# Memory stage at the head of a two-layer decoder: load order, sums of squares and the split of work over DVE and POOL changed

## The chip, the core and the metric

The kernel runs on one core of a Trainium2 chip. TensorE (PE in the profile, with its weight loads as PEld), VectorE (DVE), ScalarE (ACT), GpSimd (POOL) and SyncE (SP, whose queue issues nearly all DMAs here) run side by side, each through its own list of instructions in order, and wait for one another through semaphores. The metric is the device time of one execution in microseconds, the median of several runs.

## The reference

Two layers over 512 positions of width 1024: a gated-DeltaNet layer, then a sliding-window attention layer. Each layer also attends with four heads into 256 fixed memory rows. What the change touches is the start of it all:

```python
mem_n = rms_norm(mem, ln_mem)                 # (256, 1024)
for layer in range(DEPTH):
    h = rms_norm(x, ln_mix[layer])            # (512, 1024)
    mkv = mem_n @ w_mem_kv[layer]
    mem_k, mem_v = mkv[..., :256], mkv[..., 256:]
    ...
def rms_norm(x, g):
    y = x * rsqrt(mean(x * x, axis=-1) + EPS)
    return y * g
```

The keys and values of the memory for both layers, and the norm of x for the first layer, are therefore due before the first large projection (`h @ w_in`).

## The kernel before

**Layout.** Everything is kept transposed: the 1024 features lie as eight tiles of 128 partitions (`KD` = 8), the positions along the free axis (512 for x, 256 for mem). A product in f32 accuracy is made of three products of the faster fp32r type: each operand is split into a high part (an fp32r copy on ACT, `whi`, `mh`, `h`) and a low part (the difference, on DVE, `wlo`, `ml`, `l`), and `mm3` (L190) adds high x high, high x low and low x high. One weight tile of 128 x 1024 is a raw load (`wraw`, L173), an ACT copy and a DVE subtraction (`weight`, L179, in `parts` pieces), then 24 products.

**Norms.** The norm's factor is one number per position. `rstd_of` (L210) squares the eight feature tiles on ACT, adds them in pairs on DVE, and sums over partitions with four products by a matrix of ones on PE, in plain f32; then Ln and Exp on ACT (`rsqrt`, L205) give mean-square to the power -1/2. The factor of the memory (`mr`) is not put on mem itself: keys are multiplied by it on the way out of PSUM, values by its transpose, two columns `mc` that `memory_columns` (L373) makes on PE. The factor of x (`xr`) is multiplied into x together with the gain, one DVE instruction for each of eight tiles (`norm`, L350), then each tile is split.

**The stage.** `mem_and_norm` (L283) issues the loads on SP: gains (in `load_constants`, L258), mem in four pieces with the first key weight in two halves between them, the second key weight, the constants and a small table, x in four pieces of 512 KB, the two value weights of layer 0, `wab` (the weight of the gates), and the four memory weights of layer 1. Weight loads of the first large projection (`in_win`) follow. It then computes keys of layer 0 (two tiles in PSUM tiles `pj`), the sums of squares (PSUM `g`), values of layer 0, keys of layer 1 (PSUM `sc`), values of layer 1, and the norm of x. Results for layer 1 (`kt`) are stored to DRAM (`keep`, L380). `gates` (L392) follows with products of `h`, `l` and `wabs`, a selection by a constant matrix (`g<-consts,ab`), a short chain on DVE and ACT that ends in `gate`, and products by `gate`. Then come the projections `normed(m)`, 24 products each.

A scheduler of the language decides where each instruction stands on its engine; the order in the source is its starting point. Buffers rotate in pools: six raw weights (`wraw`), three high and three low weights, six squares (`sq`).

Of the kernel before, what the change touches and what calls it, by code (L numbers as in the profile page):

```python
# [9 lines left out]
F32 = mybir.dt.float32  # L10
# [3 lines left out]
ALU = mybir.AluOpType  # L14
# [4 lines left out]
P = 128  # L19
T = 512  # L20
D = 1024
KD = D // P
# [21 lines left out]
C_ID, C_U, C_ONE, C_CAUS, C_BAND = 0, 128, 256, 384, 512  # L44
C_SEL, C_INV, C_SIGN = 768, 780, 781
C_N = 782
# [20 lines left out]
def constants():  # L67
# [4 lines left out]
    c[:, C_ONE:C_ONE + P] = 1.0  # L72
# [13 lines left out]
class Builder:  # L86
# [123 lines left out]
    def rstd_of(self, tiles, pool, out, after=None):  # L210

        ps = self.bank("g")[:, :tiles[0].shape[1]]
        for k in range(0, KD, 2):
            two = []
            for x in tiles[k:k + 2]:
                sq = self.t(pool, [P, x.shape[1]], F32, "sq", 6)
                two.append(sq)
                ins = self.square(sq, x)
                if after is not None:
                    self.nosync(ins, after)  # L220
            self.tt(self.nc.vector, two[0], two[0], two[1], ALU.add)
            self.mm(ps, self.ones, two[0], k == 0, k == KD - 2)
        self.rsqrt(out, ps, D)
# [34 lines left out]
    def load_constants(self, cp):  # L258
# [4 lines left out]
        nc.sync.dma_start(g, a["gains"])  # L263
# [3 lines left out]
        self.ones = c[:, C_ONE:C_ONE + P]  # L267
        self.caus = c[:, C_CAUS:C_CAUS + P]
        self.band = c[:, C_BAND:C_BAND + 2 * P]
        self.one = c[:, C_ONE:C_ONE + 1]  # L270
# [12 lines left out]
    def mem_and_norm(self, ep):  # L283
# [9 lines left out]
        for k in range(0, KD, 2):  # L293
            nc.sync.dma_start(mem[:, k:k + 2, :], a["memT"][:, k:k + 2, :])
            if k < 4:
                s = slice(k // 2 * T, (k // 2 + 1) * T)
                nc.sync.dma_start(raw[0][:, s], a["wmk"][0, 0][:, s])
        raw += [early(a["wmk"][0, 1])]
        self.fetch_constants()
# [4 lines left out]
        raw += [early(s) for s in (a["wmv"][0, 0], a["wmv"][0, 1])]  # L304
        wab = self.t(ep, [P, KD, 12], F32, "wab")
        nc.sync.dma_start(wab, a["wab"])
        raw += [early(s) for s in (a["wmk"][1, 0], a["wmk"][1, 1], a["wmv"][1, 0], a["wmv"][1, 1])]
# [54 lines left out]
        keys(1)  # L362
        values(1)
        norm()
# [864 lines left out]
```

## Time and profile before

| what | value |
|---|---|
| runs of the kernel | 1167.21, 1167.46, 1170.11 us, median 1167.46 |
| the profiled execution | 1169.1 us, of which the span of the instructions is 1167.3 us |
| granted TensorE clock | 0.996 |
| PE busy | 1144.1 us |
| DVE, ACT, POOL busy | 834.2, 629.4, 82.9 us |

Rows of the timeline read: start in us, duration in us, engine, line, operation, tile written <- tiles read, shape, count, and in brackets the idle time of the engine before it with what ended it. Rows of groups give a count, then total busy us and mean ns of one, then idle time before. Rows of the table of windows give the stretch, its length, and busy time and count for PE, PEld, DVE, ACT and POOL in it, then the granted clock, the DMA share and GB/s. The chain of waits goes back from the last instruction to what released each step; its rows are start, duration, and what. Durations of products on PE include their way through the array, so the distance between two starts is what one costs.

### The profile page before, as it was taken

What the parts mean: (1) busy time and instruction counts of PE and PEld (TensorE: products, weight loads), DVE (VectorE), ACT (ScalarE), POOL (GpSimd) and SP (SyncE); (2) the same over time, 40 slices, a digit from 0 to 9 for tenths busy, and PEclk for the clock granted to TensorE, in tenths of its full rate; (3) what the DMA queues carried; (4) which work ended last, traced back from release to release, by engine and by line L of the source; (5) the groups of instructions that cost most, each with busy time, mean ns of one, the idle gap of its engine ahead of it and who ended that gap; (6) DMA issues with size and microseconds to landing.
All of it is one profiled execution on the core that took longest, in us unless ns stands there. A gap on an engine that the chain in (4) does not pass through costs nothing.

```text
span 1167.3 us, 19448 instructions
## 1 busy us (share of the span) xinstructions
PE 1144.1 (98%) x7410; PEld 999.2 (86%) x7410; DVE 834.2 (71%) x1558; ACT 629.4 (54%) x1250; POOL 82.9 (7%) x93
## 2 busy tenths in 40 slices
PE   7999999999999999999999999999999999999996
PEld 6888777877889998899998877688999988999986
DVE  6654877767788876488965768758788734889654
ACT  7579564366466642256643546865566422566433
POOL 0210000000011101011100000010011000111000
PEclk9999999999999999999999999999999999999998
DMA  8334352224557735467623421153477633776232
GB/s 306 126 110 113 114 127 92 72 91 162 163 136 187 175 102 155 123 165 180 163 79 99 129 82 55 37 126 110 100 189 183 155 99 106 168 171 172 76 99 84
DMA packets 72944, 151.22 MB, mean 130 GB/s; under 512 B 16732, under 2 KB 19444, under 8 KB 72852
## 3 DMA queue, kind: packets, MB, share of 16 engines
q1 hardware_dynamic: 61908, 130.06, 36.3%
q0 software_dynamic: 10944, 19.93, 10.9%
q8 instruction: 58, 0.95, 0.4%
q14 instruction: 34, 0.28, 0.1%
HBM read 143.00 MB, written 6.96 MB: 128 GB/s over the span
## 4 chain that ended last, share of the span: by engine, by line
PE 91%; ACT 4%; DVE 3%; DMA 1%; issue 0%; SPq 0%; DVEq 0%; ACTq 0%
PE pj L143 44%; PE g L143 39%; PE sc L143 6%; ACT sm L131 1%; PE g L147 1%; PE pt L147 1%; DVE wlo L150 1%; ACT sm L137 1%; DMA wraw<-in_wmk 1%; ACT whi L137 0%; ACT T L137 0%; PE qk L143 0%; DVE mx L743 0%; DVE sm L739 0%; DMA wraw<-in_wdn 0%
## 5 line engine op out<-in xcount | busy, mean ns | idle before, releaser
L137 ACT ACTIVATE whi<-wraw 128x512 fp32r<-128x512 f32 (+3 forms) x325 | 243.1, 754 | 292.3 <-PE pj L143 191.4
L150 DVE TENSOR_TENSOR wlo<-wraw,whi 128x512 fp32r<-128x512 f32 (+3 forms) x325 | 271.9, 845 | 109.0 <-ACT whi L137 103.5
L143 PE MATMUL pj<-h,whi 128*128 128x512 f32 (+1 forms) x676 | 265.9, 394 | 0.2
L143 PE MATMUL pj<-l,whi 128*128 128x512 f32 (+1 forms) x676 | 265.2, 392 | 0.0
L143 PE MATMUL pj<-h,wlo 128*128 128x512 f32 (+1 forms) x676 | 264.4, 392 | 0.0
L143 PE MATMUL g<-T,whi 128*128 128x256 f32 x1216 | 220.5, 282 | 0.0
L143 PEld LDWEIGHTS g<-T,whi 128*128 128x128 f32 x1216 | 187.0, 189 | 1.1 <-DVE fu L153 1.1
L143 PE MATMUL g<-T,wlo 128*128 128x256 f32 x608 | 171.1, 281 | 0.0
L143 PE MATMUL g<-h,whi 128*128 128x256 f32 (+1 forms) x516 | 152.8, 296 | 0.0
L143 PE MATMUL g<-h,wlo 128*128 128x256 f32 (+1 forms) x516 | 152.0, 295 | 0.0
L143 PE MATMUL g<-l,whi 128*128 128x256 f32 (+1 forms) x516 | 151.8, 294 | 0.0
L143 PEld LDWEIGHTS pj<-h,whi 128*128 128x128 f32 x676 | 127.1, 188 | 28.4 <-issue 2.7
L143 PEld LDWEIGHTS pj<-h,wlo 128*128 128x128 f32 x676 | 127.2, 188 | 27.2 <-issue 2.2
L143 PEld LDWEIGHTS pj<-l,whi 128*128 128x128 f32 x676 | 127.2, 188 | 26.3 <-issue 1.2
L143 PEld LDWEIGHTS g<-T,wlo 128*128 128x128 f32 x608 | 114.4, 188 | 0.0
L143 PEld LDWEIGHTS g<-h,whi 128*128 128x128 f32 x516 | 98.0, 190 | 2.9 <-issue 0.2
L143 PEld LDWEIGHTS g<-l,whi 128*128 128x128 f32 x516 | 97.9, 190 | 2.9 <-issue 0.5
L143 PEld LDWEIGHTS g<-h,wlo 128*128 128x128 f32 x516 | 98.0, 190 | 2.4
L978 POOL DMA_DIRECT2D ws<-in_wgu x38 | 33.6, 883 | 735.1 <-DVE wlo L150 335.3
L137 ACT ACTIVATE whi<-ws 128x512 fp32r<-128x512 f32 x76 | 48.0, 631 | 49.3 <-PE g L143 41.2
L150 DVE TENSOR_TENSOR fu<-pj,rstd 128x512 f32<-128x512 f32 (+1 forms) x34 | 22.4, 660 | 53.0 <-PE pj L143 53.0
L150 DVE TENSOR_TENSOR wlo<-ws,whi 128x512 fp32r<-128x512 f32 x76 | 52.1, 686 | 7.3 <-ACT whi L137 7.2
(346 smaller groups left out, 1626.0 us busy)
## 6 DMA issues: line engine op xcount, KB each, us to landing
wraw<-in_wgu SPq DMA_DIRECT2D x50, 512.0 KB, 4.1
ws<-in_wgu SPq DMA_DIRECT2D x76, 256.0 KB, 3.5
ws<-in_wgu POOLq DMA_DIRECT2D x76, 256.0 KB, 4.9
wraw<-in_win SPq DMA_DIRECT2D x26, 512.0 KB, 3.6
wraw<-in_wdn SPq DMA_DIRECT2D x32, 384.0 KB, 3.2
wraw<-in_wdn SPq DMA_DIRECT2D x32, 320.0 KB, 2.9
wraw<-in_wgu SPq DMA_DIRECT2D x38, 256.0 KB, 4.6
wraw<-in_wout SPq DMA_DIRECT2D x16, 512.0 KB, 3.6
```

The source lines that it names most:

```text
L131: ins = self.nc.scalar.activation(out, in_, func, **kw).ins
L137: self.copied = self.nc.scalar.activation(out, in_, AF.Copy, **kw).ins
L143: return self.nc.tensor.matmul(out, lhsT, rhs, start=start, stop=stop, skip_group_check=more).ins
L147: return self.nc.tensor.transpose(out, in_, self.ident[:k, :k]).ins
L150: return eng.tensor_tensor(out=out, in0=a, in1=b, op=op).ins
L978: nc.gpsimd.dma_start(s1, a22, accum_op=ALU.add)
```

## The change

Five things change, all in the first 45 us.

- **Loads.** The first piece of mem goes ahead of the gains. Both value weights of layer 0 and the first key weight of layer 1 go ahead of x; the constants and the small table go last. The matrix of ones is no longer among the constants but is set on DVE.
- **Sums of squares.** DVE adds the eight squares one after the other; PE makes one product by ones in place of four. The squares of x come after the values of layer 0.
- **The second key tile of layer 0.** Its weight is split in two halves, and its eight products with the low part of the weight stand last.
- **Low parts on POOL.** The second value weight of layer 0 gets its low part on POOL in place of DVE. (The test `j > layer` holds for that one alone.)
- **x's factors.** For four of the eight tiles, POOL multiplies x by `xr`, and the gain comes in with the split (ACT copy with a scale, DVE multiply and subtract). The norm of x stands ahead of the values of layer 1 in the source.

In the order that the scheduler makes of it, PE runs: key tile 0, key tile 1, two products of the first value tile, the product by ones for mem, ten value products, the columns, the rest of the value tiles, 18 products of layer 1's first key tile, the product by ones for x, the other layer-1 key products, 14 products of each layer-1 value tile, nine of the gates' products, two of the first projection, and then what the last value weight's low part allows: the other ten of each value tile, seven gates' products, the projections. On ACT the first value weight's copy stands behind the eight squares of mem, and a copy of a layer-1 key weight between Ln and Exp of `mr`; the last square of x stands behind the copy of the second value tile. On SP the `in_win` loads stand behind the first store of layer 1's keys.

```diff
@@ rstd_of
-        for k in range(0, KD, 2):
-            two = []
-            for x in tiles[k:k + 2]:
-                sq = self.t(pool, [P, x.shape[1]], F32, "sq", 6)
-                two.append(sq)
-                ins = self.square(sq, x)
-                if after is not None:
-                    self.nosync(ins, after)
-            self.tt(self.nc.vector, two[0], two[0], two[1], ALU.add)
-            self.mm(ps, self.ones, two[0], k == 0, k == KD - 2)
+        acc = None
+        for x in tiles:
+            sq = self.t(pool, [P, x.shape[1]], F32, "sq", 6)
+            ins = self.square(sq, x)
+            if after is not None:
+                self.nosync(ins, after)
+            if acc is not None:
+                self.tt(self.nc.vector, sq, acc, sq, ALU.add)
+            acc = sq
+        self.mm(ps, self.ones, acc)
@@ load_constants
-        nc.sync.dma_start(g, a["gains"])
-        self.ones = c[:, C_ONE:C_ONE + P]
+        self.ones = self.t(cp, [P, P], F32, "ones")
+        nc.vector.memset(self.ones, 1.0)
@@ mem_and_norm
             nc.sync.dma_start(mem[:, k:k + 2, :], a["memT"][:, k:k + 2, :])
+            if k == 0:
+                nc.sync.dma_start(self.gains, a["gains"])
...
-        raw += [early(a["wmk"][0, 1])]
-        self.fetch_constants()
+        raw += [early(s) for s in (a["wmk"][0, 1], a["wmv"][0, 0], a["wmv"][0, 1], a["wmk"][1, 0])]
...
             nc.sync.dma_start(x[:, k:k + 2, :], a["xT"][:, k:k + 2, :])
-        raw += [early(s) for s in (a["wmv"][0, 0], a["wmv"][0, 1])]
+        raw += [early(a["wmk"][1, 1])]
         wab = self.t(ep, [P, KD, 12], F32, "wab")
         nc.sync.dma_start(wab, a["wab"])
-        raw += [early(s) for s in (a["wmk"][1, 0], a["wmk"][1, 1], a["wmv"][1, 0], a["wmv"][1, 1])]
+        raw += [early(s) for s in (a["wmv"][1, 0], a["wmv"][1, 1])]
+        self.fetch_constants()
@@ keys
-                w = self.weight(None, nc.vector, raw[4 * layer + m], 1 if m + layer else 2)
+                w = self.weight(None, nc.vector, raw[4 * layer + m], 1 if layer else 2)
+                if m and not layer:
+                    s = lambda k: slice(k * P, (k + 1) * P)
+                    for k in range(KD):
+                        self.mm(ps[m], w[0][:, s(k)], mh[:, k, :], k == 0, False)
+                        self.mm(ps[m], w[0][:, s(k)], ml[:, k, :], False, False)
+                    for k in range(KD):
+                        self.mm(ps[m], w[1][:, s(k)], mh[:, k, :], False, k == KD - 1)
+                    continue
@@ values
-            w = [self.weight(None, nc.vector, raw[4 * layer + 2 + j]) for j in range(2)]
+            w = [self.weight(None, nc.gpsimd if j > layer else nc.vector, raw[4 * layer + 2 + j]) for j in range(2)]
@@ norm
-                self.stt(xk, xk, self.gain(G_MIX[0], k), xr, ALU.mult, ALU.mult)
-                self.split(xk, *self.h[k])
+                if k % 2:
+                    self.tt(nc.gpsimd, xk, xk, xr, ALU.mult)
+                    self.split_gain(xk, self.gain(G_MIX[0], k), *self.h[k])
+                else:
+                    self.stt(xk, xk, self.gain(G_MIX[0], k), xr, ALU.mult, ALU.mult)
+                    self.split(xk, *self.h[k])
@@ the order of the calls
         self.memK = keys(0)
-        self.rstd_of([x[:, k, :] for k in range(KD)], ep, xr)
         self.memory_columns(mr, mc)
         self.memV = values(0)
+        self.rstd_of([x[:, k, :] for k in range(KD)], ep, xr)
         keys(1)
+        norm()
         values(1)
-        norm()
```

More of the change, by code (lines that the diff above doesn't have):

```diff
@@ L41 @@
 G_N = G_GDN + 1
-C_ID, C_U, C_ONE, C_CAUS, C_BAND = 0, 128, 256, 384, 512
-C_SEL, C_INV, C_SIGN = 768, 780, 781
-C_N = 782
+C_ID, C_U, C_CAUS, C_BAND = 0, 128, 256, 384
+C_SEL, C_INV, C_SIGN = 640, 652, 653
+C_N = 654
 INV_FREQ = [float.fromhex(s) for s in (
@@ L71, in constants @@
     c[:, C_U:C_U + P] = i[:, None] <= i[None, :]
-    c[:, C_ONE:C_ONE + P] = 1.0
     c[:, C_CAUS:C_CAUS + P] = np.where(i[None, :] >= i[:, None], 0.0, NEG)
@@ L266, in load_constants @@
         self.U = c[:, C_U:C_U + P]
-        self.ones = c[:, C_ONE:C_ONE + P]
+        self.ones = self.t(cp, [P, P], F32, "ones")
+        nc.vector.memset(self.ones, 1.0)
         self.caus = c[:, C_CAUS:C_CAUS + P]
         self.band = c[:, C_BAND:C_BAND + 2 * P]
-        self.one = c[:, C_ONE:C_ONE + 1]
+        self.one = self.ones[:, 0:1]
         v = self.t(cp, [P, 2], F32, "eps")
```

## The prediction

> **What bounds the kernel now.** I read the page first: the span and the busy shares.
>
> ```profile
> span 1167.3 us, 19448 instructions
> PE 1144.1 (98%) x7410; PEld 999.2 (86%) x7410; DVE 834.2 (71%) x1558; ACT 629.4 (54%) x1250; POOL 82.9 (7%) x93
> ```
>
> PE is busy for all but 23.2 us, so a microsecond of PE work or PE waiting that disappears is a microsecond of the span, and other engines matter only where PE waits for them. The diff ends with the memory stage, so next I read the table of windows and the chain of waits there.
>
> ```profile
> 28.30:43.50 15.20, 15.20 (x114) 13.76 (x113) 14.56 (x21) 8.95 (x14) 3.54 (x4) 1.00 0.20 60
> ```
> ```profile
> 10.76 1.07 ACT whi L137
> ...
> 11.85 1.24 DVE wlo L150
> ...
> 13.13 2.89 PE pj L143 x22
> 16.02 6.01 PE g L143 x20
> ...
> 28.50 8.64 PE sc L143 x72
> ```
>
> From 28.3 us on PE is full. The chain shows 8.64 us for 72 products: 0.12 us from one 256-column product to the next, so about 0.24 for 512 columns. Before that the chain leaves PE at 10.76 to 13.13 (copy, then subtraction of a key weight), and spends 6 us in g, the sums of squares by ones. PE's timeline shows the pieces.
>
> ```profile
> 12.09 0.28 PE L143 MATMUL pj<-ml,whi 128*128 128x256 f32 x1
> ...
> 13.13 0.39 PE L143 MATMUL pj<-mh,wlo 128*128 128x256 f32 x1 [0.76 <-DVE wlo L150]
> ...
> 15.86 3.60 PE L143 MATMUL g<-sq,consts 128*128 128x256 f32 x12
> ```
> ```profile
> 18.44 1.02 PE L143 MATMUL g<-sq,consts 128*128 128x512 f32 x2
> ```
> ```profile
> 18.87 0.59 PE L143 MATMUL g<-sq,consts 128*128 128x512 f32 x1
> 19.39 0.60 PE L143 MATMUL g<-consts,mr 1*128 1x1 f32 x4
> ```
> ```profile
> 21.98 0.28 PE L143 MATMUL pj<-whi,ml 128*128 128x256 f32 x1
> ...
> 24.57 0.28 PE L143 MATMUL pj<-whi,mh 128*128 128x256 f32 x1
> 25.01 0.39 PE L143 MATMUL pj<-wlo,mh 128*128 128x256 f32 x1 [0.16 <-DVE wlo L150]
> ```
>
> A plain f32 product stands as two passes. Two 512-column passes start 0.43 apart (18.44, 18.87), so 256 columns take 0.215: eight of these and two of 0.43 are 2.58 us, just the distance from 15.86 to 18.44. The g stretch, 15.86 to 21.98, is 6.12 us: 8 x 0.215 + 8 x 0.43 = 5.16 of sums, 0.60 for the two columns of mr, 0.36 of waiting. PE also waits 13.13 - 12.09 - 0.12 = 0.92 for the low part of the second key weight, and 25.01 - 24.57 - 0.12 = 0.32 for that of a value weight.
>
> **The change, part by part.** Durations of the other engines, from the groups by shape within the first 50 us, and for POOL from the whole span:
>
> ```profile
> L150 DVE TENSOR_TENSOR wlo<-wraw,whi 128x1024 fp32r<-128x1024 f32 x10 | 12.2, 1223 | 4.9 <-ACT whi L137 4.8
> L137 ACT ACTIVATE whi<-wraw 128x1024 fp32r<-128x1024 f32 x10 | 10.6, 1056 | 3.0 <-PE sc L143 1.8 <-PE pj L143 0.9 <-DMA wraw<-in_wmk 0.2
> ...
> L153 DVE SCALAR_TENSOR_TENSOR x<-x,gains,xr 128x512 f32<-128x512 f32 x8 | 5.8, 746 | 0.0
> ...
> L150 DVE TENSOR_TENSOR sq<-sq,sq 128x512 f32<-128x512 f32 x4 | 2.8, 692 | 2.7 <-ACT sq L140 2.7
> ...
> L150 DVE TENSOR_TENSOR sq<-sq,sq 128x256 f32<-128x256 f32 x4 | 1.6, 422 | 0.2 <-ACT sq L140 0.2
> ...
> L137 ACT ACTIVATE whi<-wraw 128x512 fp32r<-128x512 f32 x2 | 1.2, 612 | 0.0
> ```
> ```profile
> L150 POOL TENSOR_TENSOR DT<-gcr,consts 128x512 f32<-128x512 f32 x6 | 8.5, 1458 | 10.6 <-DMA gcr<-dr 10.6
> ...
> L150 POOL TENSOR_TENSOR T<-T,ws 128x512 f32<-128x512 f32 x2 | 2.6, 1284 | 89.0 <-ACT ws L131 89.0
> ```
>
> (1) One product by ones in place of four, for mem and for x: six 256-column and six 512-column passes go, 6 x 0.215 + 6 x 0.43 = **3.87 us of PE work removed**. The 0.36 of waiting among them goes too.
>
> (2) The second key weight is cut in halves and its low products stand last. The copy halves end at about 11.4 and 11.9 (0.61 each from 10.76), the low halves on DVE (0.69 each) at 12.1 and 12.7. PE ends the first key tile at 12.0 and has 16 high products, to 13.9, before it needs a low part. The wait of 0.92 goes; the tile ends at 14.85 instead of 15.86. With the 0.32 above, whose place in the new order is worked out in (4), the removed waits are 0.92 + 0.36 + 0.32 = **1.6 us**.
>
> (3) Loads. The memory weights stand ahead of x on SP, the constants last.
>
> ```profile
> GB/s 0 38 139 227 193 326 338 389 375 400 304 311 390 373 426 414 426 407 417 417 406 410 414 414 410 348 205 20 0 0 0 0 36 103 0 125 6 8 131 0
> ```
> ```profile
> 5.46 0.91 ACT L137 ACTIVATE mh<-mem,gains 128x256 fp32r<-128x256 f32 x2 [3.44 <-DMA mem<-in_memT]
> ...
> 17.79 0.47 ACT L131 ACTIVATE mr<-g,eps 128x256 f32<-128x256 f32 x1
> ```
> ```profile
> 17.87 1.61 SPq L176 DMA_DIRECT2D wraw<-in_win  x2
> 32.06 3.06 SPq L384 DMA_DIRECT2D mk<-kt  x2
> ```
> ```profile
> wraw<-in_win SPq DMA_DIRECT2D x26, 512.0 KB, 3.6
> ```
>
> The row of rates (40 slices of 1 us) runs near 410 GB/s, 1.28 us for 512 KB. Both orders bring the second key weight at 10.7; then come the value weights at 12.0 and 13.3, a layer-1 key weight at 14.6, x at 15.9, 17.1, 18.4 and 19.7, the rest by about 25. Constants are first read near 41 us (gates), the ones now come from a DVE memset: both cost nothing. Gains swap places with the first part of mem, and the first ACT copy needs both: between 0.44 earlier (one issue slot, mem's) and 0.3 later; I take 0, since the same bytes are ahead of the pair. The win loads fall behind the store of mk on SP. That store waits for the first layer-1 key tile, near 27.5; a load then takes 3.6 us, so the first is there at 31.5 and the second at 32.3, and ACT's copies of them stand behind the fourth h, which ends at 32.6: covered, by a microsecond or less.
>
> (4) New waits. ACT is in order:
>
> ```profile
> 11.72 2.55 ACT L140 ACTIVATE sq<-mem 128x256 f32<-128x256 f32 x8
> ```
>
> A: the eight squares (2.55) start at 11.8 and end at 14.35, the value weight's copy behind them at 15.35; PE, done at 14.85, waits 0.5. B: seven dependent adds of 0.42 + 0.02 on DVE run from 12.6 to 15.7, after which PE's one product takes 0.43, to 16.15 (wait 0.1); the value weight's low part stands behind the adds on DVE, 15.6 to 16.85: PE waits 0.7. The columns need Ln 0.47, a layer-1 key copy of 1.06 that stands between, and Exp: 18.1, where PE arrives as well (0.05). C: the second value weight's low part is now on POOL. It starts at 16.3; 128x1024 is not in the trace, twice the 512 rows gives 2.57 to 2.92, ending 18.9 to 19.2, and PE asks at 18.95: 0 to 0.3, I take 0.15. New waits so far 0.5 + 0.1 + 0.7 + 0.05 + 0.15 = **1.5**. The lead at layer 1's first key product is 3.87 + 1.6 - 1.5 = 4.0 us; x's product (0.86) is still to come there, so this product moves from 28.5 to about 23.6.
>
> The Trainium skill ("GPSIMD Engine Reference", Performance versus the Vector engine) gives POOL 1.96 times DVE's time for an f32 tensor_tensor; on DVE's 1.223 that would be an estimated 2.40 us, C would be 0 and the sum 0.15 better.
>
> x's chain: the eighth square queues on ACT behind the second value tile's copy, which waits for PE until 23.6; its add ends at 25.4, and PE, 18 products further, asks for the sum at 25.8: covered, by 0.4. Then 0.86 on PE, Ln, a weight copy, Exp: xr at 29.0. D: half of x's factors move to POOL (four times 1.28 to 1.46, from 29.0 to 34.8 at most). DVE saves four of 0.746. It still has, in this order from 28.4, a value weight's low part, two x, a kt (as the 256-column add, 0.42), four l, two x and the last value weight's low part. On DVE instructions overlap:
>
> ```profile
> 36.00 1.89 DVE L150 TENSOR_TENSOR l<-x,h 128x512 fp32r<-128x512 f32 x3
> ```
>
> Three of 0.69 in 1.89: 0.09 at each border. So 2 x 1.223 + 6 x 0.746 + 2 x 0.69 + 0.42 = 8.7, less 0.9 at ten borders, ends near 36.2. PE, with 12.5 us of products behind 23.6, asks for that low part at 36.1. DVE beside POOL:
>
> ```profile
> 55.47 8.53 POOL L150 TENSOR_TENSOR DT<-gcr,consts 128x512 f32<-128x512 f32 x6 [10.56 <-DMA gcr<-dr]
> ```
> ```profile
> 57.73 1.36 DVE L150 TENSOR_TENSOR wlo<-wraw,whi 128x1024 fp32r<-128x1024 f32 x1 [0.89 <-ACT whi L137]
> ```
>
> With POOL at work the subtraction took 1.36 instead of 1.223, 11% more; on 5 us of overlap that is 0.5. So D is between 0.1 and 1.2 (the stretch doubled); I take **0.5**. E, the gates:
>
> ```profile
> 45.56 0.51 PE L143 MATMUL pj<-l,whi 128*128 128x512 f32 x1
> 45.91 0.40 PE L143 MATMUL pj<-h,wlo 128*128 128x512 f32 x1
> ```
> ```profile
> 47.99 0.18 DVE L153 SCALAR_TENSOR_TENSOR gate<-gate,ea 128x24 f32<-128x24 f32 x1
> ```
>
> From the end of the gates' selection (45.56) to the gate (48.17) are 2.6 us; the new order puts 8 products of about 0.24 there, 1.9 us: a wait of 0 to 0.7, I take **0.3**. F: a change between plain f32 and fp32r products costs 0.35 - 0.24 = 0.1 (45.56 to 45.91). The sums now stand in three places instead of one: two more visits, 0 to 0.4, **0.2**.
>
> Sum: 4.0 - 0.5 - 0.3 - 0.2 = **3.0 us** off. The profiled execution took 1169.1 (span 1167.3 and 1.8 around it), so it would be 1166.1; it stands 1.6 above the median of the runs, 1167.46, from which the same 3.0 gives **1164.5**. I carry the lead to the end in full, since PE's other waits start from results that come earlier by as much. Bounds of the unknown costs: best 4.0 + 0.15 + 0.44 - 0.1 = 4.5, so 1163.0; worst 4.0 - 0.15 - 0.3 - 1.2 - 0.7 - 0.4 = 1.25, so 1166.2.
>
> **The rivals.** (R1) More than the sum: A and B do not come to pass. Both hang on a DVE chain of seven adds and on ACT's place for one copy; were these a microsecond earlier, PE would find its operands, and 3.0 + 1.2 = 4.2 gives 1163.3, with the best of the other bounds 1161.9. Against it: ACT's 2.55 us of squares are a row, and they stand ahead of the copy. (R2) The lead is swallowed: the win loads issued ten microseconds later, or x's chain with its 0.4 of cover, become the wait. Each microsecond that one is late is lost; 2 to 3 us late, which a load of 3.6 that meets others can be, gives 1166.5 to 1167.5. For it: the covers of a microsecond and less; against: the row of rates falls to 0 at 28 us, the queue is empty there. (R3) Slower: DVE and POOL shut each other out of SBUF for a whole instruction. Then in D each of POOL's four multiplications holds DVE, whose operations all have two SBUF inputs, for 1.28 to 1.46 us: 5.1 to 5.8 on a chain without slack. 4.0 - 0.3 - 0.2 - (5.1 to 5.8) is 1.6 to 2.3 us slower: 1169.1 to 1169.8, and more if POOL waits for DVE as well. It decides from 3.5 us of lost DVE time on. Against it: the subtraction at 57.73 began in the middle of six POOL operations without a break and took 0.13 longer, no POOL operation's length.
>
> The rule behind R3 is the Trainium skill's ("SBUF — State Buffer", Who interferes with whom): a DVE instruction with two SBUF inputs and a GpSimd one that reads SBUF exclude each other, "an exclusive lock". By that rule 57.73 should have waited for the running POOL operation; the trace doesn't show it.
>
> **How the numbers follow.** Forecast 0.58, R1 0.15, R2 0.17, R3 0.10. The likeliest is 1164.5, with its own range of 1163.0 to 1166.2; taking in R2 and most of R1, 1162.0 to 1167.4 leaves out under 2 in 10. About 0.3%, 3.5 us, is what a measurement of this kernel can tell from no change: faster is under 1163.96, slower over 1170.96. Faster: R1's 0.15 and a little under half of the forecast, 0.27, so 0.42. Slower: half of R3, 0.05. Within: 0.53.
>
> **What would show it.** Right: two products by ones of two passes each; no wait at the second key tile; waits of 0.5 and 0.7 for a value weight's copy and low part near 15 and 17 us; layer 1's first key product near 24 us, the gates' selection, now at 44.6, near 41.5. Wrong: POOL's operations at 2 us or more per 512 columns, or DVE idle or stretched beside them (R3); ACT waiting for in_win (R2); a layer-1 start before 23 (R1); a gap in PE after 50 us that the profile of before has not.

## The result, and the profile after

The changed kernel takes 1170.03 us (median of 22 runs, 1169.15 to 1171.43), the kernel before in the same sessions 1168.07 (22 runs). The ratio is 1.0018, 95% interval 1.0012 to 1.0024: 2.0 us slower. That lies inside the 0.3% that were called no change, but the forecast of 3.0 us faster is wrong, and so is its range. The profiles below show one execution each; that of the changed kernel is the slowest of its 22, 1171.43 us.

The page of the changed kernel, its span and busy times:

```profile
span 1169.6 us, 19446 instructions
PE 1143.2 (98%) x7398; PEld 998.2 (85%) x7398; DVE 840.3 (72%) x1561; ACT 629.2 (54%) x1251; POOL 93.0 (8%) x98
```

The removed products are gone (twelve matmul records fewer), but busy time falls by 0.9 us only, where 3.9 were taken out. Busy time is no measure of work here: it also counts what slower products take longer (those at the start, 0.21 us apart, last until 14.2 us, before until 11), and each product's way through the array ahead of a wait. PE's timeline of the changed kernel shows where it stood still (in brackets the idle time before, and what ended it):

```profile
9.06 0.41 PE L142 MATMUL pj<-mh,wlo 128*128 128x256 f32 x1
10.49 0.58 PE L142 MATMUL pj<-mh,whi 128*128 128x256 f32 x1 [1.01 <-ACT mh L136]
...
17.41 0.70 PE L142 MATMUL g<-sq,ones 128*128 128x256 f32 x2 [0.33 <-DVE sq L149]
18.55 0.39 PE L142 MATMUL pj<-wlo,mh 128*128 128x256 f32 x1 [0.44 <-DVE wlo L149]
...
25.19 0.28 PE L142 MATMUL sc<-mh,whi 128*128 128x256 f32 x1
...
27.95 1.13 PE L142 MATMUL g<-sq,ones 128*128 128x512 f32 x2 [0.45 <-DVE sq L149]
...
37.16 0.45 PE L142 MATMUL pj<-l,wabs 128*64 128x512 f32 x1 [0.91 <-DVE l L149]
38.85 0.45 PE L142 MATMUL pj<-l,wabs 128*64 128x512 f32 x1 [1.01 <-DVE l L152]
...
41.44 0.68 PE L142 MATMUL pj<-h,wabs 128*64 128x512 f32 x1 [0.87 <-ACT h L136]
...
48.74 0.61 PE L142 MATMUL g<-consts,ab 64*128 64x12 f32 x4
```

Layer 1's first key product stands at 25.19 (before 28.34, forecast 23.6), so the first part did gain, 3.15 us. The gates' selection stands at 48.74 (before 44.58, forecast 41.5): that stretch is 7.3 us longer, where the forecast had 1.7 (17.9 against 16.24). The table of windows, from the one product to the other, of the kernel before and after:

```profile
28.34:44.58 16.24, 16.24 (x119) 14.30 (x117) 14.52 (x21) 9.73 (x16) 4.62 (x4) 1.00 0.23 69
```
```profile
25.19:48.74 23.55, 20.32 (x122) 16.08 (x120) 20.63 (x24) 13.62 (x22) 9.43 (x8) 0.93 0.20 68
```

PE had no idle time there before and 3.2 us (23.55 - 20.32) after; DVE was busy for 14.5 us and is now for 20.6; the granted clock fell to 0.93. What DVE did in that stretch, and POOL beside it, is in the timeline of the changed kernel:

```profile
31.92 3.49 DVE L152 SCALAR_TENSOR_TENSOR x<-x,gains,xr 128x512 f32<-128x512 f32 x2
35.33 0.41 DVE L149 TENSOR_TENSOR kt<-sc,mr 128x256 f32<-128x256 f32 x1
35.67 1.44 DVE L149 TENSOR_TENSOR l<-x,h 128x512 fp32r<-128x512 f32 x1
37.03 1.76 DVE L152 SCALAR_TENSOR_TENSOR l<-x,gains,h 128x512 fp32r<-128x512 f32 x1
38.71 0.68 DVE L149 TENSOR_TENSOR l<-x,h 128x512 fp32r<-128x512 f32 x1
```
```profile
17.46 3.28 POOL L149 TENSOR_TENSOR wlo<-wraw,whi 128x1024 fp32r<-128x1024 f32 x1 [16.20 <-ACT whi L136]
31.35 6.90 POOL L149 TENSOR_TENSOR x<-x,xr 128x512 f32<-128x512 f32 x4 [10.61 <-ACT xr L130]
```

While POOL multiplies (31.35 to 38.25), two of DVE's x take 3.49 instead of 1.41, an l 1.44 instead of 0.69, the next 1.76 instead of 0.75; at 38.71, POOL being done, an l takes 0.68 again. Only kt, which has one of its inputs in PSUM, is as short as ever (0.41). That is what rival R3 named.

### The profile page after: what moved, and what is told of

Read it like the earlier page. It is cut to its first block, busy times and chain, and to the rows that moved or that the text cites. A ratio compares the mean times of both kernels' runs of the same rounds, so it can differ in the third digit from the quotient of the medians.

```text
span 1169.6 us, 19446 instructions
## 1 busy us (share of the span) xinstructions
PE 1143.2 (98%) x7398; PEld 998.2 (85%) x7398; DVE 840.3 (72%) x1561; ACT 629.2 (54%) x1251; POOL 93.0 (8%) x98
## 4 chain that ended last, share of the span: by engine, by line
PE 90%; DVE 4%; ACT 4%; issue 1%; DMA 1%; SPq 0%; DVEq 0%; ACTq 0%
PE pj L142 45%; PE g L142 38%; PE sc L142 5%; ACT sm L130 1%; DVE wlo L149 1%; PE g L146 1%; PE pt L146 1%; ACT sm L136 1%; DMA mem<-in_memT 1%; ACT whi L136 1%; PE qk L142 0%; DVE x L152 0%; DVE btmp L149 0%; DVE mx L757 0%; DVE sm L753 0%
## 5 line engine op out<-in xcount | busy, mean ns | idle before, releaser
L149 DVE TENSOR_TENSOR wlo<-wraw,whi 128x512 fp32r<-128x512 f32 (+3 forms) x325 | 272.4, 847 | 106.4 <-ACT whi L136 100.2
L149 DVE TENSOR_TENSOR fu<-pj,rstd 128x512 f32<-128x512 f32 (+1 forms) x34 | 22.4, 660 | 55.0 <-PE pj L142 55.0
L149 DVE TENSOR_TENSOR wlo<-ws,whi 128x512 fp32r<-128x512 f32 x76 | 52.1, 686 | 7.3 <-ACT whi L136 7.2
```

Of the source, the lines that this page charges most:

```text
L149: return eng.tensor_tensor(out=out, in0=a, in1=b, op=op).ins
```

## The experiments

All medians are beside runs of the kernel before in the same session, and ratios are to it. Where a line number is given, L149 is `tt`, L152 is `stt`.

**1. x's factors back on DVE.**

```diff
-                if k % 2:
-                    self.tt(nc.gpsimd, xk, xk, xr, ALU.mult)
-                    self.split_gain(xk, self.gain(G_MIX[0], k), *self.h[k])
-                else:
-                    self.stt(xk, xk, self.gain(G_MIX[0], k), xr, ALU.mult, ALU.mult)
-                    self.split(xk, *self.h[k])
+                self.stt(xk, xk, self.gain(G_MIX[0], k), xr, ALU.mult, ALU.mult)
+                self.split(xk, *self.h[k])
```

> The changed kernel with all eight of x's factors on DVE again, the rest of the change kept. Lock (POOL's four multiplications and DVE's instructions shut each other out): after 31.9 us DVE is busy for 13.1 us with pieces that alone would take 9.2; with all factors on DVE the same stretch is 11.7. So no DVE operation of 512 columns is over 0.76 us, the gates' selection comes 1.4 us earlier than 48.7 or, if the clock does not fall to a half at 42 us, 2.7 earlier, and the time is 1167.3 to 1168.6, 1.4 to 2.7 under the changed kernel. Late sum (x's factor xr is ready at 31.3 instead of 24.2, and DVE simply has too much to do behind it, with or without POOL): the four multiplications come back onto DVE, 2.6 us more, the selection is at 50 to 51 and the time 1171 to 1172.6.

Measured: 1169.65 (1168.13 to 1170.75), ratio 1.0013 (1.0004 to 1.0021). No instruction of x's stretch is longer than 0.75, and the profile's selection is at 45.62, 3.1 earlier than in the changed kernel. Of this, 1.1 was there already at layer 1's first key product (24.05, not 25.19): mem's third part was copied at 8.63 in this profile and at 9.93 in the other. That is chance, the loads being the same. The other 2.0 is less than the 2.7 that the lock theory gave for a clock that stays, as it did in this profile. The median, though, is only 0.4 us under the changed kernel, less than that theory said. POOL still had the low part of the value weight, and its rows carry on the story:

```profile
16.33 3.27 POOL L149 TENSOR_TENSOR wlo<-wraw,whi 128x1024 fp32r<-128x1024 f32 x1 [15.07 <-ACT whi L136]
```
```profile
18.47 2.22 DVE L149 TENSOR_TENSOR wlo<-wraw,whi 128x1024 fp32r<-128x1024 f32 x1 [1.11 <-ACT whi L136]
```

DVE's subtraction at 18.47 lasts 2.22 instead of 1.22; POOL's ends at 19.6, and 1.1 later DVE's.

**2. Gains ahead of mem again.**

```diff
+        nc.sync.dma_start(g, a["gains"])
...
-            if k == 0:
-                nc.sync.dma_start(self.gains, a["gains"])
```

> The changed kernel with the gains loaded ahead of the first part of mem again, all other loads as changed. Loads (the swap lets PE start at 6.24 instead of 6.94, but mem's third and fourth part land at 9.9 and 10.6 instead of 8.8 and 9.5, PE runs dry for a microsecond and its products take 0.21 us instead of 0.12 until 14.2): mem's fourth part lands near 9.5, the products are at 0.12 from about 11, layer 1's first key product comes 1.1 us earlier than 25.2, and the time is 0.5 to 1.6 under the changed kernel, 1168.4 to 1169.5. Rival (the value weights queued behind, or chance, make the third part late, not the gains): it lands at 9.9 again, and the time is within 0.3 of the changed kernel.

Measured: 1170.33 (1168.80 to 1172.40), ratio 1.0018 (1.0010 to 1.0027). Mem's third part was there earlier, PE ran through without the pause at 9, and layer 1's first key product came at 24.31, 0.9 earlier. The time did not follow, against the first theory: what the swap may be worth is lost in the interval of a microsecond, and it is not what made the kernel 2.0 us slower.

**3. The kernel before, with x's odd factors on POOL.** The edit in `norm` is the reverse of experiment 1.

> The kernel before with one edit, every second factor of x on POOL. Lock: POOL's operations of 512 columns take 1.6 us or more, DVE's beside them 1.4 or more instead of 0.75; four of POOL's operations cost DVE 3.6 us and save it 2.6, so DVE ends the stretch about 1 us later than 42.9; PE has waited for nothing there, so the time is 0 to 2 above the kernel before. Contention of 11% (the row at 57.73): DVE's operations beside POOL take 0.83, POOL's 1.46, DVE ends the stretch about 2 us earlier, and the time is that of before within 0.3.

Measured: 1171.80 (1170.71 to 1173.37), ratio 1.0033 (1.0020 to 1.0045), 3.7 us slower, above what either theory said. Rows of POOL, DVE and PE in this kernel:

```profile
25.25 7.45 POOL L150 TENSOR_TENSOR x<-x,xr 128x512 f32<-128x512 f32 x4 [23.99 <-ACT xr L131]
```
```profile
25.82 1.78 DVE L153 SCALAR_TENSOR_TENSOR x<-x,gains,xr 128x512 f32<-128x512 f32 x1
27.53 2.33 DVE L150 TENSOR_TENSOR wlo<-wraw,whi 128x1024 fp32r<-128x1024 f32 x1
29.78 1.77 DVE L150 TENSOR_TENSOR l<-x,h 128x512 fp32r<-128x512 f32 x1
31.48 1.77 DVE L153 SCALAR_TENSOR_TENSOR l<-x,gains,h 128x512 fp32r<-128x512 f32 x1
33.17 0.74 DVE L153 SCALAR_TENSOR_TENSOR x<-x,gains,xr 128x512 f32<-128x512 f32 x1
```
```profile
35.10 0.39 PE L143 MATMUL sc<-mh,wlo 128*128 128x256 f32 x1 [2.06 <-DVE wlo L150]
```

Four instructions of DVE stand beside four of POOL, and each is longer than its own time by 1.02 to 1.11, whatever its own time is (0.75, 1.22, 0.69, 0.75). A share of bandwidth would stretch the long ones more; a lock adds the same to each. PE paid in one place that the expectation had not seen: it waited 2.06 us for the low part of a memory weight, queued behind. And then the granted clock (the third column from the end) fell to a half for some 3.4 us:

```profile
36.00:38.00 2.00, 2.00 (x13) 2.00 (x12) 2.00 (x5) 0.14 (x1) 0.00 (x0) 0.57 0.02 6
38.00:40.00 2.00, 2.00 (x12) 2.00 (x12) 2.00 (x4) 0.92 (x1) 0.00 (x0) 0.58 0.18 64
```

At half the clock that is an estimated 1.7 us more (half of 3.4). This execution took 1173.37; the two of the five with the highest granted clock, 0.998, took 1170.71 and 1171.18, so without the fall the price is about 3 us.

**4. The kernel before, with one product by ones behind seven adds**, at the old places (`rstd_of` as changed).

> The kernel before with one edit, one product by ones behind seven dependent adds, for mem and for x at their old places. PE work: 3.9 us less, so 1163.6 if all of it is kept. Chain of adds: x's last piece lands at 17.9, its squares end near 19.2, and with the adds of 0.78 one behind the other the sum is ready near 20.6 to 21; PE, which would ask at about 17, waits 3 to 4 us there, so that the value products start near 21.5 as before and the time is within 0.7 of the kernel before, 1167.4 to 1168.8.

Measured: 1172.12 (1171.28 to 1172.36), ratio 1.0034 (1.0022 to 1.0046), 4.0 us slower, above what either theory said.

```profile
22.13 2.08 PE L143 MATMUL g<-sq,consts 128*128 128x512 f32 x2 [4.69 <-DVE sq L150]
```
```profile
22.00:26.00 4.00, 3.87 (x10) 2.35 (x11) 2.52 (x4) 1.90 (x5) 0.00 (x0) 0.50 1.02 408
```

The chain took more than the products had cost: PE stood for 4.69 us at x's sum. The clock fell to a half in that wait and stayed there until 28.7, with products of 256 columns 0.21 us apart instead of 0.12: 6.5 us of work that would take an estimated 3.7 (6.5 x 0.12 / 0.21), so most of the 4.0 lost is the clock's. So x's sum had to move behind the values in the change, where PE has other work.

**5. Four runs on order and on the sums.** In order: the changed kernel with `norm()` behind `values(1)` again; the same without POOL (the factors as in experiment 1, and the edit below); that one with the four adds and four products of before; and the kernel before with the second key weight in halves and its low products last.

```diff
-            w = [self.weight(None, nc.gpsimd if j > layer else nc.vector, raw[4 * layer + 2 + j]) for j in range(2)]
+            w = [self.weight(None, nc.vector, raw[4 * layer + 2 + j]) for j in range(2)]
```

> The changed kernel with x's factors behind layer 1's values again, the rest kept, POOL's share too. Order (with the factors ahead, nine of the gates' sixteen products stand on PE ahead of twenty of layer 1's value products, and PE waits for l and h with work in hand): the value products cover the wait, the gates' selection comes 2 to 3 us earlier, near 46 to 46.5 with mem on time, and the time is 2 to 3 under the changed kernel, 1167 to 1168. DVE bound (DVE is busy without a break from 30 to 45 in any order and its last l sets the selection): the selection stays at 47.5 or later, and the time within 0.7 of the changed kernel.

> The changed kernel without POOL's work (all eight factors and the low part of the second value weight on DVE) and with x's factors behind layer 1's values. Lock and order together: no DVE operation is stretched, PE waits only for the sum of x; the selection is at 44 to 45 with mem on time, the time 1166.5 to 1168, some 2 to 3.5 under the changed kernel. DVE bound by the adds (seven dependent adds each for mem and x cost DVE 9.1 us where the four plain adds cost 4.4): DVE has 4.7 us more to do than in the kernel before and none of it is taken off, PE waits for l, the selection is at 46 or later and the time at 1168.5 or more.

> As the run without POOL and with the factors last, and with the sums of squares of the kernel before, four adds and four products by ones each: what is left of the change is the order of the loads, x's sums behind layer 0's values, and the low parts of the second key tile last. DVE bound: the 3.9 us that PE pays again are given back by 4.7 us of DVE, the selection is at 43.5 to 44.5, and the time 1166 to 1167.5, at or under the run with one product each. PE bound: the four products cost 3.9 us, the selection is at 47 to 48, and the time 2 to 4 above the run with one product each.

> The kernel before with one edit, the second key weight copied in halves and its low products last. All of the 0.9 us wait at 12.1 to 13.1 goes and PE is 0.9 earlier from there on: time 0.9 under the kernel before, 1167.2. Swallowed: mem's sums by ones are then 0.9 earlier than their adds (the last add ends at 14.7, the first at 13.4), and x's squares, whose loads end at 17.9, make the products by ones of x wait instead: time within 0.3 of before.

Measured: norm last 1169.67, ratio 1.0014 (1.0006 to 1.0023). Without POOL and norm last **1166.32**, ratio 0.9988 (0.9980 to 0.9996), under the kernel before. With four products 1166.74, 0.9994 (0.9985 to 1.0002). Before with the low products last 1168.21, 1.0009 (1.0000 to 1.0018).

The order theory is not borne out by the time: the factors' place alone moved nothing that can be told from 0. (The profile of that run has the selection at 46.19, as the order theory said, but it is of the fastest of its eleven executions, 1168.11.) Without POOL and with one product the change does make the kernel faster; with four products it cannot be told from the kernel before, nor from the run with one. The 3.9 us of PE work against DVE's longer adds is close to an even trade. The low products last bring nothing alone: PE is at mem's sum at 14.90 instead of 15.86, but x's sum keeps it, and the first value product comes at 21.60 instead of 21.46.

**6. POOL's two jobs, one at a time, and the adds as trees.** First the changed kernel without any POOL work; then with the low part on DVE and the factors on POOL; then without POOL, norm last, and

```diff
-            if acc is not None:
-                self.tt(self.nc.vector, sq, acc, sq, ALU.add)
-            acc = sq
-        self.mm(ps, self.ones, acc)
+            two.append(sq)
+            if len(two) == 4:
+                self.tt(self.nc.vector, two[0], two[0], two[1], ALU.add)
+                self.tt(self.nc.vector, two[2], two[2], two[3], ALU.add)
+                self.tt(self.nc.vector, two[0], two[0], two[2], ALU.add)
+                self.mm(ps, self.ones, two[0], x is tiles[3], x is tiles[7])
+                two = []
```

> The changed kernel without POOL's work, factors and low part on DVE, with x's factors ahead of layer 1's values as changed. It stands between the run with the factors on DVE (1169.65, low part on POOL) and the run without POOL and with the factors last (1166.32). Low part (POOL's subtraction of 1024 columns held DVE's for 1.0 us at 18.5 and everything behind it): x's sum is 1.2 us earlier than 26.8, and the time is 1.0 to 1.5 under the run with the factors on DVE, 1168.2 to 1168.7, the other 2 us being the order. Order costs nothing: 1166.3 as with the factors last. Low part costs nothing: 1169.6.

> The changed kernel with the low part of the second value weight on DVE again, x's odd factors still on POOL and ahead of the values. Low part: x's sum 1.2 us earlier, PE still waits three times for l and h between 34 and 42, time 1168.8 to 1169.0, 1.0 to 1.2 under the changed kernel. If the wait for l and h is set by DVE's total work and not by the start of x's sum: the selection stays at 47.5 and the time at 1169.7 to 1170.3.

> No POOL, factors last, and the sums of squares as two products by ones behind two trees of three adds each, so that no add waits for more than one other. PE pays one more product for mem (0.43) and for x (0.86), DVE's adds take 6 of 0.39 and 6 of 0.66 instead of 9.1 us in two chains, 2.8 less. Chain theory (the dependent adds set when x's factor is ready and DVE's end): the waits of 0.7 at 16.4, 0.4 at 25.9 and 1.1 at 40.0 go, 0.9 more than PE pays: 1165.4. PE theory: 1.3 more than the run with one product, 1167.6.

Measured: no POOL 1166.03, ratio 0.9984 (0.9974 to 0.9993). Low part on DVE, factors on POOL: 1167.33, 0.9998 (0.9989 to 1.0007). Two products: **1165.27**, 0.9979 (0.9970 to 0.9988). The second of these is under both of its expectations, so the low part weighed more than any of the theories had it; the first says that the order costs nothing without POOL; the third fits the chain theory, though its interval overlaps that of one product in the same order (0.9988, 0.9980 to 0.9996).

From 1.0018 to 0.9984 POOL's work costs 0.0034, 4.0 us, give or take 1.3 by the intervals. By itself the low part, put at 0.15 in the prediction, is worth 0.0020 to 0.0029, 2.3 to 3.4 us (with the factors on POOL, and with them on DVE), and the factors 0.0005 to 0.0014. For the factors DVE's balance fits: 3.8 us lost beside POOL (rows above) against four multiplications of 0.75 saved. For the low part it doesn't: 1.0 lost, 1.22 saved. But there the scheduler's order changed as well: with the low part on POOL and the factors ahead, the last ten products of each of layer 1's value tiles stand behind most of the gates' products on PE, with the low part on DVE ahead of all of them. On DVE the low part of layer 1's last value weight, which those ten begin with, stands behind x's first tiles in the one (at 41.31 in the changed kernel) and ahead of them in the other (done by 31.4 with only the factors on POOL).

**7. The lock alone.** Two kernels like the one without POOL, with work for POOL that nobody reads; the lists of PE, DVE and ACT are the same in the same order. A third puts the gains first in the kernel with two products.

```diff
+            for k in range(4):
+                idle = self.t(ep, [P, 2, ML], F32, "idle", 2)
+                xr2 = xr.rearrange("p (a b) -> p a b", a=2)
+                self.tt(nc.gpsimd, idle, mem[:, 2 * k:2 * k + 2, :], xr2, ALU.mult)
```
```diff
+            if not layer:
+                idle = self.t(ep, [P, D], F32, "idle")
+                self.tt(nc.gpsimd, idle, raw[3], w[1][0].bitcast(F32), ALU.subtract)
```

> The run without POOL's work (1166.03), with four multiplications of 512 columns on POOL that nobody reads: pieces of mem by xr into a tile of their own, as soon as xr is there. The instructions on PE, DVE and ACT and their order are the same. Lock: each of the four holds a DVE instruction with two inputs in SBUF for 1.0 to 1.1 us, DVE ends the stretch 4.2 us later, PE waits for l where it has no other work, and the time is 2 to 4 us above, 1168 to 1170. No lock (what the runs with POOL lost was the order and the longer way of x's odd tiles): the time is 1165.5 to 1166.6.

> The run without POOL's work (1166.03), with one subtraction of 1024 columns on POOL that nobody reads, of the second value weight and its high part, where the changed kernel makes the low part. Order on PE, DVE and ACT as without it. Lock alone: POOL's instruction takes 2.3 to 3.3 us, DVE's subtraction behind it 2.2 instead of 1.2, the sum of x comes 1.0 later, time 1166.6 to 1167.2. If the order that the scheduler makes when the low part stands on POOL is what cost the most (2.3 to 3.4 us in all by the runs so far), this run shows no more than the 1.0; if the lock does it all, it is at 1168.3 or more.

> The fastest run so far (two products by ones behind trees of adds, no POOL, factors last; 1165.27), with the gains loaded ahead of mem as in the kernel before. Loads: in its profile PE waits 1.1 us at 9.0 for mem's third part, which gains first takes away: 1164.2 to 1164.8. Chance: no part of that wait is due to the gains, 1165.0 to 1165.6.

Measured: four idle multiplications 1168.93, ratio 1.0016 (1.0007 to 1.0025), against 0.9984 without them: 3.7 us for results that no one uses. The idle subtraction 1167.66, 1.0000 (0.9991 to 1.0008), 1.9 us, between the 1.0 expected if the order had cost the most and the 2.3 expected if the lock did it all. Gains first 1164.88, 0.9976 (0.9966 to 0.9985), not to be told from 0.9979.

Rows of the kernel without POOL, and of the one with idle multiplications, where DVE makes the same three x:

```profile
31.53 2.07 DVE L152 SCALAR_TENSOR_TENSOR x<-x,gains,xr 128x512 f32<-128x512 f32 x3
```
```profile
32.08 4.58 DVE L152 SCALAR_TENSOR_TENSOR x<-x,gains,xr 128x512 f32<-128x512 f32 x3
36.58 1.78 DVE L149 TENSOR_TENSOR l<-x,h 128x512 fp32r<-128x512 f32 x1
```

And POOL and DVE of the one with the idle subtraction:

```profile
16.43 3.26 POOL L149 TENSOR_TENSOR idle<-wraw,whi 128x1024 f32<-128x1024 f32 x1 [15.16 <-ACT whi L136]
```
```profile
17.37 3.41 DVE L149 TENSOR_TENSOR wlo<-wraw,whi 128x1024 fp32r<-128x1024 f32 x1
```

DVE's subtraction of 1.22 takes 3.41, held for 2.2 us, nearly all of POOL's time. In the run with the multiplications DVE is held for 2.51 (three x) and 1.09 (an l), 3.6 in all, and the time is 3.7 longer; in the other 2.2, and 1.9. With no order changed, the lock alone thus costs about what it holds (each difference is good to 1.5 us), because DVE has no slack here.

**8. The low part on POOL where the order stays.** In the kernel without POOL and with the factors last, and in the one with two products, the second value weight's low part goes back to POOL (the one-line edit of experiment 5 reversed). Two products on PE change place; the value products all stay ahead of the gates'.

> The run without POOL and with the factors last (1166.32, ratio 0.9988), with the low part of the second value weight on POOL. The order on PE is all but the same (two products in another place), unlike between the changed kernel and the run with that low part on DVE, where 19 of layer 1's value products went behind the gates' products. Order theory (the low part cost 2.3 to 3.4 us because of that): here it costs no more than DVE's balance, 1.0 held against 1.22 saved, so 1166.0 to 1166.8. Lock theory (it costs 2 to 3 us by itself, through x's sum): 1168.3 to 1169.5.

> The run with two products behind trees (1165.27, ratio 0.9979), with the low part of the second value weight on POOL; again the order on PE differs in one place only. Order theory: 1165.0 to 1165.8. Lock theory: 1167 to 1168.5.

Measured: 1167.45, ratio 0.9995 (0.9986 to 1.0004), against 0.9988 with the low part on DVE, between the two theories; and 1165.77, 0.9979 (0.9970 to 0.9988), against 0.9979, as the order theory has it. With the order kept, POOL's subtraction cost 0 to 0.8 us, less than its 2.3 to 3.4 in experiment 6. The ratios by what stands on POOL and where the norm of x stands:

| on POOL | norm ahead of layer 1's values | norm behind them |
|---|---|---|
| low part and factors | 1.0018 | 1.0014 |
| low part | 1.0013 | 0.9995 |
| factors | 0.9998 | not run |
| nothing | 0.9984 | 0.9988 |

With the low part alone on POOL the order is worth 0.0018, good to 0.0012 by the two intervals, or 2.1 us. With both jobs on POOL, as in the change, it is worth 0.0004, nothing that can be told from 0. The value products do stand ahead of the gates' there, but the low part that they wait for is made beside POOL's multiplications, takes 2.30 instead of 1.22, and PE waits for it:

```profile
32.86 2.30 DVE L149 TENSOR_TENSOR wlo<-wraw,whi 128x1024 fp32r<-128x1024 f32 x1
```
```profile
35.21 0.39 PE L142 MATMUL sc<-wlo,mh 128*128 128x256 f32 x1 [1.65 <-DVE wlo L149]
```

So it is shown that POOL's two jobs cost 4.0 us in the change, that the lock costs time by itself, and that the order can cost 2 us beside the low part. How the 4.0 us divide between lock and order in the change itself stays open. The first run of this experiment differs from the run with the norm last (1.0014) by the factors alone: 0.0019, 2.2 us, that POOL's four multiplications cost there.

## Why the prediction was wrong

**The failed step is D**, what POOL's work does to DVE's chain. "With POOL at work the subtraction took 1.36 instead of 1.223, 11% more; on 5 us of overlap that is 0.5", and R3 was put at 0.10 because at 57.73 no instruction was held. The row is right and was read from one side. These are single instructions of POOL in the kernel before, the one beside that subtraction and one with nothing of DVE beside it:

```profile
57.97 2.29 POOL L150 TENSOR_TENSOR DT<-gcr,consts 128x512 f32<-128x512 f32 x1
...
61.47 1.28 POOL L150 TENSOR_TENSOR DT<-gcr,consts 128x512 f32<-128x512 f32 x1
```

DVE came 0.24 us ahead of the border between two of POOL's instructions, took its turn there, and POOL waited: 2.29 instead of 1.28, a microsecond more, nearly DVE's whole 1.22. The mean of the group that the prediction quoted, 1458 ns for six, hides it: five of 1.29 and one of 2.29. The DVE instructions around it (`kn<-pj,gains,kn`) ran beside POOL without harm, but one of their inputs is in PSUM. So the trace of before held R3's evidence, on the other engine. That DVE was let through there was luck. In the changed kernel the subtraction at the same place came just behind the start of one of POOL's, took 2.24, and PE stood for 0.77 behind it, where it had no idle time before:

```profile
61.35 1.29 POOL L149 TENSOR_TENSOR DT<-gcr,consts 128x512 f32<-128x512 f32 x1
```
```profile
61.48 2.24 DVE L149 TENSOR_TENSOR wlo<-wraw,whi 128x1024 fp32r<-128x1024 f32 x1 [0.96 <-ACT whi L136]
```
```profile
66.67 0.66 PE L146 MATMUL g<-consts,kn 128*128 128x128 f32 x4 [0.77 <-ACT kn L130]
```

That is the "gap in PE after 50 us" which the prediction had named as a sign of being wrong. The Trainium skill's rule ("SBUF — State Buffer", Who interferes with whom), that DVE instructions with two SBUF inputs and GpSimd ones that read SBUF exclude each other, agrees with all these rows; the prediction had set it aside.

**What D measured.** It had DVE's chain "near 36.2" at the low part of the last value weight, just when PE asks. That subtraction ended at 42.5:

```profile
41.31 1.21 DVE L149 TENSOR_TENSOR wlo<-wraw,whi 128x1024 fp32r<-128x1024 f32 x1
```

Of the 6.3 us, 2.3 are the start (`xr` was ready at 31.3, not 29.0), and 2.08 + 0.75 + 1.01 = 3.8 are DVE's loss beside the four multiplications (the rows after, against 1.41, 0.69 and 0.75), where 0.5 was taken and 1.2 was the worst bound. In the order of the changed kernel PE has most of the gates' products ahead of the last ten of each value tile, which begin with that low part, so it stood still for l and h. The range could not hold the time, since its bounds were bounds of contention. Between the forecast, 3.0 faster, and the result, 2.0 slower, lie 5.0 us: POOL's work cost 4.0, which is 3.35 more than the 0.65 that D and C had booked; the other 1.65 are a lead that came out short, as said below.

**C** was wrong in size and nearly without weight: POOL's low part took 3.28 us, not 2.57 to 2.92, since it waited for DVE's running subtraction, and held DVE's next for 1.0. Its place on POOL also changed the order, which the prediction had read and not charged to it; what that cost in the change itself is not shown (experiment 8).

**R3** held the measured 2.0 us in its 1.6 to 2.3. Its mechanism is shown, its sum is not: it set the whole price against a lead of 4.0 kept to the end, and gave the order no part. That the number fits is luck. R1 did not come, with layer 1's start at 25.19. (By its own terms R1's lower end is 1161.8, not 1161.9.)

**(1) came, and the lead came out short.** The products went. Layer 1's first key product came 3.15 us earlier in the changed kernel, 4.03 with the gains first (24.31); the forecast of 23.6 was 4.7. Without POOL the change is 1.9 us under the kernel before (0.9984; 0.8 to 3.0 by the interval), where the sum had 3.0.

**(2)** The wait of 0.9 at the second key tile went, but experiment 5 shows it alone to be worth nothing: it is taken up again at x's sum.

**(3) Loads, costed at 0: not quite.** "The same bytes are ahead of the pair" held for the first copies, which came 0.7 earlier, not for what is behind: mem's third part, at 8.86 on ACT before, was copied at 9.93 in the changed kernel, and PE ran dry at 9.06. Over all profiles it was copied at 7.83 to 8.86 with the gains first (six, 8.5 on average) and at 8.59 to 9.96 with them second (twelve, 9.2 on average), so the profile of the changed kernel is one of the late ones. No effect on the time could be measured (experiment 2). ACT waited 0.81 for a win load at 51.94, but PE for nothing there, as forecast; R2 did not come.

**(4)** B came, smaller: the value weight's low part kept PE for 0.44 by the row at 18.55, forecast 0.7. A did not come, as PE itself was later. The seven adds of mem took 3.60 us (forecast 3.1), those of x 5.48. In the chain the adds of 256 columns start 0.53 us apart (13.76, 14.28, 14.81); in the kernel before, where none needs the one ahead of it, 0.35 (12.99, 13.33, 13.69). So an add that needs the one ahead of it starts nearly 0.2 later, where the prediction took 0.02 on top of its 0.42. x's sum, "covered, by 0.4", kept PE waiting for 0.45. The trees of experiment 6 fit this: fewer dependent adds, and the lowest medians, though not by more than the intervals.

**The lead carried to the end in full** cannot be read off the two profiles. Near 140 us PE meets a wait for the layer's softmax. The table of windows there, of the kernel before and after:

```profile
138.00:140.40 2.40, 0.35 (x2) 0.02 (x1) 2.33 (x9) 2.38 (x7) 0.00 (x0) 1.00 0.00 0
140.40:142.00 1.60, 1.58 (x7) 1.33 (x8) 1.60 (x7) 1.59 (x5) 0.00 (x0) 0.62 0.00 0
142.00:144.00 2.00, 2.00 (x9) 1.17 (x9) 1.86 (x6) 1.36 (x4) 0.00 (x0) 0.50 0.00 0
```
```profile
142.60:144.30 1.70, 0.35 (x2) 0.00 (x0) 1.66 (x6) 1.68 (x5) 0.00 (x0) 1.00 0.00 0
144.30:146.00 1.70, 1.67 (x11) 1.23 (x12) 1.70 (x7) 1.69 (x5) 0.00 (x0) 1.00 0.00 0
```

In the profiled execution of before PE stood still for 2.1 us and the clock then fell to a half; in that of after it stood for 1.4, and the clock stayed. So the two spans differ by 2.3 us only, though PE was 4.6 later before it (the first product of qm and mk at 135.25 against 130.65). This is not a lead that is swallowed. In all 14 profiles of the changed kernel and its variants the wait is 1.36 to 1.39 us, whether PE comes early (that first product at 128.47) or late (135.25). In the four of the kernel before and its variants it is 2.06, 1.82, 1.39 and 2.63, and why is open. The clock fell behind the two waits of over 2 us and behind none of the other 16. The prediction had taken one profiled execution, with such a fall in it, for the rule.

## What to carry to other kernels

Where DVE and POOL both read SBUF, POOL takes its time out of DVE's: look for it in single instructions of both engines where they overlap, since it shows on the one that came second, as a longer instruction and not as idle time, and a mean over a group hides it. DVE's instructions with an input in PSUM were exempt here. Read also the order that the scheduler makes of a move, and ask what stands behind each product that may have to wait; in one pair of runs here that cost 2.1 us, more than the moved subtraction itself. Work taken from PE pays only as far as the chain that replaces it is covered: one product behind seven adds cost 4.0 us where PE had to wait for it, and a tree of adds that pays one product back was at least as fast as the chain.

## What the runs showed of the hardware

- The lock's length is not POOL's duration. In experiment 3 each of DVE's instructions was held for 1.02 to 1.11 us by a POOL instruction of 512 columns that takes 1.28 alone, and for 2.2 by one of 1024.
- It needs reads on both sides. `kt`, with an input in PSUM, took its usual 0.41 beside POOL, and in the kernel without POOL's arithmetic, POOL's memsets (from 36.85 on, some 5 us) left three x beside them at 2.07 and three l at 1.89.
- An idle stretch of PE can be paid twice. After the waits at 36 to 42 the granted clock of the changed kernel fell to a half, as it did behind a single wait of 2.06 us in experiment 3 and in one of 4.69 in experiment 4. It did not in the run with idle multiplications, where PE waited for 3.1 us between 37 and 46.5 in pieces of under 0.9. The changed kernel:

```profile
36.00:42.00 6.00, 3.21 (x11) 1.18 (x10) 6.00 (x7) 3.83 (x7) 2.24 (x2) 0.96 0.07 23
42.00:44.00 2.00, 2.00 (x9) 1.67 (x8) 2.00 (x4) 1.13 (x2) 0.00 (x0) 0.50 0.00 0
```

- At the start the products of 256 columns are 0.21 us apart, and 0.12 later. In the changed kernel the step came at 14.2, after the pause at 9 to 10.5; in the kernel before, without that pause, at 11. The column of the granted clock shows 1.00 in both, so there only the spacing tells.
